# Moving one norm and thirteen projection steps earlier in a woven single-core transformer layer

## The chip, the cores and the metric

The kernel runs on one core of a Trainium2 chip. The metric is the device time of one execution in microseconds (us); the time of a kernel is the median of several executions. The engines are named as in the profile: PE (TensorE matmul) and PEld (its weight loads), DVE (VectorE), ACT (ScalarE), POOL (GpSimd, which here only issues gathers) and SP (SyncE, which issues all other transfers). An L and a number is a line of the kernel.

## The reference, cut to what matters

One layer over 1,024 tokens of width 1,024. The tokens are handled in blocks of 128, numbered 0 to 7.

```
xn     = rmsnorm(x, norm1_w)
proj   = xn @ w_in           # 52 column tiles of 128: q, k, v of two attentions, and two gates
o_d    = diff_attention(...) # 8 heads, two softmax maps each, chunk-causal
o_c    = chunk_attention(...)# 8 heads, band of 9 chunks of 64
merged = sigmoid(gd) * (o_d @ w_branch_diff) + sigmoid(gc) * (o_c @ w_branch_chunk)
h      = x + merged @ w_out
q      = rmsnorm(h, norm2_w) @ peer_wq       # then scores against two key tables
e, g   = the 16 best experts of 8 heads, and their softmax weights
y      = rmsnorm(h + sum_e g * gelu(u[e] . xn2) * v[e], final_norm_w)
```

## The kernel before, in words

Blocks are projected in two groups (L31): group 0 is blocks 0 and 1, group 1 is blocks 2 to 7 (768 tokens).

**Norm.** `norm1(gi, xp)` (L212) normalises a group block by block and yields after each. A block is one 512 KB load of `x` into a slot of the ring `wr`, a square with sum on ACT (L222), five tiny ACT operations for the reciprocal root (L113 to L118), a scaled copy (L224) into a slot of the ring `wl`, eight transposes on PE (L203), and eight pairs of an ACT copy (L231, `xh`) and a DVE subtraction (L232, `xl`), which split the value into a high and a low part.

**Projection steps.** `Dense` (L236) holds the 52 steps of a group. A step loads one 512 KB weight tile into `wr`, splits it on ACT (L126, `wh`) and DVE (L127, `wl`), multiplies it on PE in 24 products for every 512 tokens or part of them (L134; group 1 has a part of 512 and one of 256 tokens), copies the result on ACT into `st`, and SP stores it to DRAM (L287, L296, L302). `upto(n)` emits steps until n are emitted, `run()` emits one for each `next`. The ring `wr` has three slots and is shared by the norm's `x`, the steps' raw weights and the weights of the merges; `wh`, `wl` have two slots, `st` three.

**Attention.** `att_one` (blocks 0 and 1, one at a time) and `att_pair` (blocks 2 and 3) yield 12 and 24 times; they call `need`, which emits the projection steps that the next head needs, if they are not yet emitted. Attention reads k, v and q back from DRAM.

**Merge and selection.** `merge` (L478) yields 25 times: eight products with the two branch weights and gates (L505 to L511), eight with `w_out` and a transpose (L516 to L521), the second norm (L528 to L534), and eight query products with scores (L540 to L553) whose 16 best are found by DVE (`top16`, L558). `choose` (L565), called by `sel`, combines them on DVE in nine pieces and ends with the expert list `ei` of the block.

**Order.** `weave(main, n, (g, m))` (L52) advances `main` and, after its i-th piece, brings the side generator `g` to m * min(i, n) // n pieces; what is left of a side is emitted when `main` ends. The program order around the change is: norm of group 0; attention of block 0 woven with the rest of group 0's steps; merge of block 0 woven with attention of block 1; selection of block 0; merge of block 1 woven with the norm of group 1; selection of block 1; six steps of group 1; attention of blocks 2 and 3 woven with the other 46.

```
weave(merge(mp, 0, [0], yza, *ons[0]), 25, (att_one(wk, 1, yz1), 13))
run(sel([0], yza))
weave(merge(mp, 0, [1], yz1, *ons[1]), 25, (norm1(1, x1), 6))
...
run(sel([1], yz1))
```

Program order is not the order of issue. The kernel is built with a scheduler that runs a model of time over the whole program: an instruction that is earlier in the program goes first, and a later one whose inputs and buffers are there fills in. What comes out is a fixed order on each engine and queue. In the trace, for instance, gathers of `experts` (L790, called last of all) are issued by POOL between the pieces of merge 1.

**The rest.** Attention of blocks 4 to 7 with the merge of 2 and 3, gates and merges of the others, the selection of blocks 6 and 7, and then `dense_experts` (L681): blocks 2 to 5 go through all experts as 128 chunks of matrix products on PE. Blocks 0, 1, 6 and 7 (`experts`) gather 128 rows of `u` and 128 of `v` per block (L804, 512 KB each, five slots `ge`), which DVE reduces one by one (L810 for `u`, L816 for `v`).

## Time and profile before

| | us |
|---|---|
| time, median of three executions | 3437.65 (3435.08 to 3438.16) |
| the profiled execution, its own time | 3433.26 |
| its span, first to last instruction | 3431.5 |
| PE busy in the span | 3085.0 (90%) |
| DVE busy | 2700.0 (79%) |
| ACT busy | 1446.3 (42%) |
| POOL busy | 1249.1 (36%) |

The profiled execution is one of its own, some 4 us under the median of the three timed ones. A share of busy time is a mean over stages: PE has no idle time in some of them and waits in others. All positions in time below are us from the start of the span.

### The profile page before, as it was taken

What the parts mean: (1) busy time and instruction counts of PE and PEld (TensorE: products, weight loads), DVE (VectorE), ACT (ScalarE), POOL (GpSimd) and SP (SyncE); (2) the same over time, 40 slices, a digit from 0 to 9 for tenths busy, and PEclk for the clock granted to TensorE, in tenths of its full rate; (3) what the DMA queues carried; (4) which work ended last, traced back from release to release, by engine and by line L of the source; (5) the groups of instructions that cost most, each with busy time, mean ns of one, the idle gap of its engine ahead of it and who ended that gap; (6) DMA issues with size and microseconds to landing.
All of it is one profiled execution on the core that took longest, in us unless ns stands there. A gap on an engine that the chain in (4) does not pass through costs nothing.

```text
span 3431.5 us, 48288 instructions
## 1 busy us (share of the span) xinstructions
PE 3085.0 (90%) x16032; PEld 2551.8 (74%) x16032; DVE 2700.0 (79%) x5848; ACT 1446.3 (42%) x3029; POOL 1249.1 (36%) x1028
## 2 busy tenths in 40 slices
PE   7987699999979886987798359999999999999998
PEld 7986578888857654676677348888888888888886
DVE  4436897777779899987976978889998888999543
ACT  5634433434423544567669523333233333333332
POOL 0000455555544522344000144555555555555000
PEclk9999899999989987998898669999999999999999
DMA  7675999999999975898544499999999999999531
GB/s 240 219 244 189 374 333 348 333 352 334 326 340 351 324 236 186 281 360 331 203 162 157 145 343 319 346 350 339 347 345 345 346 342 344 346 340 349 166 123 49
DMA packets 406122, 987.13 MB, mean 288 GB/s; under 512 B 43184, under 2 KB 188400, under 8 KB 403696
## 3 DMA queue, kind: packets, MB, share of 16 engines
q0 software_dynamic: 147456, 536.94, 44.1%
q1 hardware_dynamic: 258416, 447.11, 37.4%
q8 instruction: 126, 2.06, 0.2%
q14 instruction: 124, 1.02, 0.1%
HBM read 905.72 MB, written 78.15 MB: 287 GB/s over the span
## 4 chain that ended last, share of the span: by engine, by line
PE 71%; issue 12%; DVE 7%; DMA 7%; ACT 2%; POOL 1%; SPq 0%; DVEq 0%; POOLq 0%; ACTq 0%
PE ph L134 20%; PE mm L134 16%; PE acc L710 15%; PE acc L717 5%; PE mm L490 5%; PE sc L347 3%; PE pv L372 3%; PE tr L203 2%; DMA ge<-in_u_dram,ei 2%; DVE junk L810 1%; DVE p L353 1%; POOL ge L804 1%; DMA rb<-rst 1%; DMA ge<-in_v_dram,ei 1%; DVE acc L816 1%
## 5 line engine op out<-in xcount | busy, mean ns | idle before, releaser
L804 POOL DMA_INDIRECT ge<-in_u_dram,ei x512 | 619.1, 1209 | 1249.0 <-DVE junk L810 396.4
L804 POOL DMA_INDIRECT ge<-in_v_dram,ei x512 | 629.8, 1230 | 683.2 <-DVE acc L816 462.0
L816 DVE SCALAR_TENSOR_TENSOR acc<-ge,a,acc 128x1024 f32<-128x1024 f32 x512 | 655.1, 1280 | 26.2 <-DMA ge<-in_v_dram,ei 20.1
L810 DVE SCALAR_TENSOR_TENSOR junk<-ge,xs 128x1024 bf16<-128x1024 f32 x512 | 624.7, 1220 | 53.7 <-DMA ge<-in_u_dram,ei 45.7
L127 DVE TENSOR_TENSOR wl<-wr,wh 128x1024 fp32r<-128x1024 f32 x232 | 283.6, 1223 | 233.1 <-ACT wh L126 107.5
L126 ACT CAST wh<-wr 128x1024 fp32r<-128x1024 f32 x232 | 243.7, 1051 | 406.5 <-PE ph L134 267.1
L134 PE MATMUL ph<-x2h,wh 128*128 128x512 f32 x1024 | 400.3, 391 | 11.8 <-ACT wh L126 10.4
L134 PE MATMUL ph<-x2l,wh 128*128 128x512 f32 x1024 | 399.9, 390 | 0.0
L134 PE MATMUL mm<-xh,wh 128*128 128x256 f32 (+1 forms) x1248 | 372.0, 325 | 0.7 <-ACT st L286 0.5
L134 PE MATMUL mm<-xl,wh 128*128 128x256 f32 (+1 forms) x1248 | 366.8, 321 | 1.4 <-DVE xl L232 1.3
L134 PEld LDWEIGHTS mm<-xh,wh 128*128 128x128 f32 x1248 | 236.9, 190 | 24.8 <-ACT st L286 2.3
L134 PE MATMUL ph<-x2h,wl 128*128 128x512 f32 x1024 | 253.1, 389 | 0.0
L134 PEld LDWEIGHTS mm<-xl,wh 128*128 128x128 f32 x1248 | 236.4, 190 | 21.5 <-DVE xl L232 2.1
L126 ACT CAST vh<-vr 128x512 fp32r<-128x512 f32 x256 | 140.4, 619 | 264.8 <-PE acc L717 243.4
L134 PE MATMUL mm<-xh,wl 128*128 128x256 f32 (+1 forms) x1248 | 234.4, 323 | 0.0
L134 PEld LDWEIGHTS ph<-x2h,wh 128*128 128x128 f32 x1024 | 193.2, 189 | 52.9 <-ACT wh L126 10.8
L134 PEld LDWEIGHTS ph<-x2l,wh 128*128 128x128 f32 x1024 | 193.2, 189 | 40.2
L134 PEld LDWEIGHTS ph<-x2h,wl 128*128 128x128 f32 x1024 | 192.3, 188 | 40.0
L347 PE MATMUL sc<-kt,qt 64*128 64x256 f32 (+3 forms) x608 | 202.1, 533 | 17.8 <-DVE mn L353 10.2
L710 PE MATMUL acc<-vh,ah 128*128 128x512 f32 x768 | 198.3, 389 | 0.0
L126 ACT CAST ah<-ge 128x512 fp32r<-128x512 f32 x128 | 79.7, 622 | 281.4 <-DVE ge L757 266.3
L134 PEld LDWEIGHTS mm<-xh,wl 128*128 128x128 f32 x1248 | 184.7, 189 | 16.8
(199 smaller groups left out, 5741.6 us busy)
## 6 DMA issues: line engine op xcount, KB each, us to landing
vr<-in_v_dram SPq DMA_DIRECT2D x128, 512.0 KB
wr<-in_ut_dram SPq DMA_DIRECT2D x128, 512.0 KB
wr<-in_w_in_dram SPq DMA_DIRECT2D x104, 512.0 KB
gdr<-gst SPq DMA_DIRECT2D x16, 2048.0 KB
gj<-gdr SPq DMA_DIRECT2D x512, 64.0 KB
wr<-in_w_bd_dram SPq DMA_DIRECT2D x40, 512.0 KB
wr<-in_w_out_dram SPq DMA_DIRECT2D x40, 512.0 KB
wr<-in_wq_dram SPq DMA_DIRECT2D x40, 512.0 KB
```

The lines of the kernel that those rows point to most:

```text
L126: nc.scalar.copy(hi, raw)
L127: nc.vector.tensor_sub(lo, raw, hi.bitcast(F32))
L134: nc.tensor.matmul(o, w[a][:, k, :], xx[b][:, k, :], start=(i == 0), stop=(i == last))
L203: nc.tensor.transpose(o[:, i * P:(i + 1) * P], s, ident)
L347: nc.tensor.matmul(o[:, :k1 - k0], q, k[:, k0:k1], start=True, stop=True)
L372: nc.tensor.matmul(o[:, :P], aT[:, j - c, :], vt[:, v0 + j, :], start=(j == 0), stop=(j == n - 1))
L490: nc.tensor.matmul(o, w[:, k, :], xx[:, k, :], start=(k == 0), stop=(k == K - 1))
L710: nc.tensor.matmul(acc[i][hf], a[x][:, i * P:(i + 1) * P], b[y][:, hf * 512:hf * 512 + 512], **kw)
L717: nc.tensor.matmul(o, aa[:, 3 * P:4 * P], bb[:, cs], start=(n == 0), stop=(n == len(todo) - 1))
L804: nc.gpsimd.indirect_dma_start(out=t, out_offset=None, in_=src, in_offset=bass.IndirectOffsetOnAxis(ap=ei[:, k:k + 1], axis=0))
L810: nc.vector.scalar_tensor_tensor(junk, t, 1.0, xs, op0=OP.mult, op1=OP.mult, accum_out=hid[:, k:k + 1])
L816: nc.vector.scalar_tensor_tensor(acc, t, a[:, k:k + 1], acc, op0=OP.mult, op1=OP.add)
```

## The change

`norm1(1)` is chained behind the remaining steps of group 0 as a side of block 0's attention, so its six blocks follow those steps (by the weave's counts two of them before that attention has ended and four when it has), instead of being spread over the merge of block 1. A new generator `some(n)` emits n steps, one per `next`. Group 1's steps come as sides: 2 over the merge of block 0, 4 over the selection of block 0, 3 over the merge of block 1 and 4 over the selection of block 1, which makes 13. The six steps ahead of `att_pair` fall away, and its side has 39 steps left instead of 46. Instructions, sizes, buffers and pools are the same as before; only the program order differs.

```diff
--- before.py
+++ after.py
@@ -262,6 +262,11 @@
             while self.done < min(n, len(self.steps)):
                 self.steps[self.done]()
                 self.done += 1
+
+        def some(self, n):
+            for _ in range(n):
+                self.upto(self.done + 1)
+                yield
 
         def run(self):
             while self.done < len(self.steps):
@@ -877,15 +882,14 @@
                 dn[0].upto(3)
                 setup()
                 dn[0].upto(6)
-                weave(att_one(wk, 0, yza), 13, (dn[0].run(), 46))
+                weave(att_one(wk, 0, yza), 13, (chain(dn[0].run(), norm1(1, x1)), 52))
             with pool("mp0") as mp:
-                weave(merge(mp, 0, [0], yza, *ons[0]), 25, (att_one(wk, 1, yz1), 13))
-                run(sel([0], yza))
-                weave(merge(mp, 0, [1], yz1, *ons[1]), 25, (norm1(1, x1), 6))
-            run(sel([1], yz1))
+                weave(merge(mp, 0, [0], yza, *ons[0]), 25, (att_one(wk, 1, yz1), 13), (dn[1].some(2), 2))
+                weave(sel([0], yza), 9, (dn[1].some(4), 4))
+                weave(merge(mp, 0, [1], yz1, *ons[1]), 25, (dn[1].some(3), 3))
+            weave(sel([1], yz1), 9, (dn[1].some(4), 4))
         with wpool("at1") as wk:
-            dn[1].upto(6)
-            weave(att_pair(wk, 1, yza), 25, (dn[1].run(), 46))
+            weave(att_pair(wk, 1, yza), 25, (dn[1].run(), 39))
     with pool("yzb") as yzb, pool("mp") as mp:
         d1 = [k for k in range(ND) if DBLK[k] < 4]
         d2 = [k for k in range(ND) if DBLK[k] >= 4]
```

## Rows read from the trace of the kernel before

**Rows 1.** The page: busy time per engine, and the granted clock in 40 slices.
```profile
PE 3085.0 (90%) x16032; PEld 2551.8 (74%) x16032; DVE 2700.0 (79%) x5848; ACT 1446.3 (42%) x3029; POOL 1249.1 (36%) x1028
...
PEclk9999899999989987998898669999999999999999
```

**Rows 2.** Busy by stretch: length, PE, PEld, DVE, ACT, POOL, clock, DMA share, GB/s.
```profile
195.00:435.00 240.00, 174.27 (x1194) 153.18 (x1195) 153.73 (x627) 98.76 (x297) 45.93 (x42) 0.88 0.79 278
...
960.00:1680.00 720.00, 615.99 (x3148) 460.52 (x3149) 637.76 (x1773) 386.40 (x924) 270.23 (x243) 0.90 0.84 296
1680.00:1925.00 245.00, 194.42 (x1066) 169.14 (x1066) 189.91 (x804) 177.65 (x408) 0.00 (x0) 0.87 0.44 158
...
2010.00:3190.00 1180.00, 1169.55 (x5146) 967.85 (x5147) 1048.30 (x1372) 370.62 (x558) 616.61 (x482) 0.99 0.96 343
...
340.00:435.00 95.00, 56.29 (x357) 50.56 (x356) 75.70 (x246) 41.38 (x117) 45.32 (x42) 0.82 0.97 370
...
519.00:960.00 441.00, 440.68 (x2602) 369.40 (x2600) 334.75 (x512) 173.78 (x370) 236.51 (x193) 1.00 0.95 339
```

**Rows 3.** What PE waited for from 195 to 435 us: total us, times, longest.
```profile
PE tr L203 <- ACT xs L224: 18.3, 4, 7.1
PE tr L203 <- DVE xs L530: 10.6, 2, 6.5
PE mm L490 <- DMA wr<-in_w_bd_dram: 7.2, 5, 2.9
PE sc L547 <- ACT st L542: 6.7, 4, 5.1
```

**Rows 4.** Timeline of PE: first products of two successive projection steps; first of att_pair.
```profile
473.60 0.39 PE L134 MATMUL mm<-xh,wh 128*128 128x512 f32 x1
...
482.02 0.39 PE L134 MATMUL mm<-xh,wh 128*128 128x512 f32 x1
...
519.41 1.77 PE L347 MATMUL sc<-kt,qt 64*128 64x384 f32 x6
```

**Rows 5.** Timeline of PE: sixteen equal products of merge 1 at two clocks.
```profile
322.56 2.02 PE L490 MATMUL mm<-on,wr 128*128 128x128 f32 x16 [1.72 <-DVE ohib L617]
...
328.41 3.65 PE L490 MATMUL mm<-on,wr 128*128 128x128 f32 x16 [2.93 <-DMA wr<-in_w_bd_dram]
```

**Rows 6.** Groups of instructions by form, 325 to 453 us: busy us, mean ns, idle before.
```profile
L231 ACT ACTIVATE xh<-tr,w1c 128x128 fp32r<-128x128 f32 x48 | 16.9, 367 | 28.2 <-DVE xl L232 22.3 <-PE tr L203 4.0 <-issue 1.2
...
L232 DVE SCALAR_TENSOR_TENSOR xl<-tr,w1c,xh 128x128 fp32r<-128x128 f32 x48 | 15.6, 343 | 3.9 <-ACT xh L231 3.3 <-issue 0.2
...
L224 ACT ACTIVATE xs<-xt,nr 128x1024 f32<-128x1024 f32 x6 | 6.9, 1148 | 0.2
L222 ACT ACTIVATE xs<-xt 128x1024 f32<-128x1024 f32 x6 | 6.3, 1058 | 6.9 <-DMA xt<-in_x_dram 6.8
...
L114 ACT ACT_TABLE_LOAD x1 | 1.3, 1283 | 0.0
```

**Rows 7.** What SP's queue waited for: 300 to 435 us (first row), 435 to 600 us.
```profile
SPq L487 <- ACT xs L224: 13.4, 4, 3.8
...
SPq L287 <- ACT st L286: 36.2, 13, 9.5
SPq L296 <- ACT st L292: 17.9, 4, 5.9
```

**Rows 8.** Line L804 (the gathers) by stretch; line L810; POOL's last instruction.
```profile
435.00:960.00 525.00, 280.81 (x228) 1.00 0.95 338
960.00:1680.00 720.00, 270.23 (x243) 0.90 0.84 296
...
L810 DVE SCALAR_TENSOR_TENSOR junk<-ge,xs x512: 1196/1220/1280, 346.4 to 2888.4; 128x1024 bf16<-128x1024 f32 x171
L810 DVE DVE_READ_ACCUMULATOR junk<-ge,xs x512: 70/82/89, 347.5 to 2889.6; 128x1 f32 x171
...
3180.41 1.14 POOL L804 DMA_INDIRECT ge<-in_v_dram,ei  x1 [2.99 <-DVE acc L816]
```


## The prediction

> **What bounds the kernel now.** I read the page first: PE is busy nine tenths of the span, DVE eight, and the granted clock leaves full speed only in some slices [rows 1]. So the question is where PE waits. The table of busy time by stretch answers it [rows 2]. From 519 to 960 us, while group 1 is projected, PE has no gap (440.68 of 441 us), and the dense experts from 2010 to 3190 us are full too (1169.55 of 1180). Between them lie stretches in which PE is idle a seventh to a fifth of the time. The change touches the first stretch with gaps, 195 to 435 us, in which blocks 0 and 1 are merged and selected: PE is busy 174.27 of 240 us, so 65.7 us idle, and 38.7 of these lie in the last 95 us (340 to 435), where merge 1, the norm and the first gathers run together. What ended these gaps stands in [rows 3]: first the norm's own transposes, for which PE stands 18.3 us until ACT has scaled the block; then the second norm of the merges (10.6), weights of the first products on their way (7.2), and the query copies on ACT (6.7). The gap belongs to the path: what follows, 519 to 960 us, is PE without a hole, so a microsecond of projection that fits into a gap ahead of it is a microsecond less there. At the far end nothing takes it away: POOL's last gather is issued at 3180 us [rows 8], 250 us before the end of the span, and PE's dense chunks are the last to finish.
>
> **The change part by part.** *The thirteen steps.* One step of group 1 takes PE 8.42 us: the first product of one stands at 473.60 us, that of the next at 482.02 us [rows 4]. Nine steps (2 + 4 + 3) come ahead of the end of merge 1, so 9 x 8.42 = 75.8 us of PE work is added to the stretch with the gaps, and the same 75.8 us leaves the full stretch behind it. The last four, over selection 1, replace the six that stood there before and ran under the same DVE work; that exchange I cost at nothing, since the steps left over for the attention of blocks 2 and 3 fill PE as soon as their buffers are free, as they do now until the first product of that attention at 519.41 us [rows 4]. If that cover is gone, PE waits for the end of selection 1, at most two steps, 17 us. So the gain is the part of the 65.7 us of gaps that the nine steps fill, between 0 (they only lengthen the stretch by 75.8) and 65.7.
>
> *How much is filled.* The 18.3 us at the norm's transposes I count in full: the transposes no longer stand in PE's queue among merge 1's products. Of the other 47.4 us I take half, 23.7. Speaking for more: the steps interleave product by product with whatever is ready. Against: PE's order is fixed by a model of time, and gaps that the model does not foresee (late weights, DVE held by a gather) stay gaps whatever is placed behind them. Sum 42.0.
>
> *The clock.* The stretch has a mean granted clock of 0.82 to 0.88, against 1.00 in the full ones [rows 2]. Sixteen equal products of merge 1 take 2.02 us behind a short wait and 3.65 us behind a long one [rows 5], the first at the level of 2.4 GHz, the second mostly at 1.2. Each such case costs 1.6 us. The mean of 0.88 over 240 us is about 58 us at the lower level, mostly gaps; if a seventh of it is work, 8 us are lost. I take 4 of them back; bounds 0 and 8.
>
> *The norm, moved.* It leaves merge 1: 30.1 us of ACT (L231 16.9, L224 6.9, L222 6.3) and 15.6 us of DVE [rows 6]. It also leaves the ring `wr`: SP held merge 1's weights 13.4 us until L224 had let go of a slot [rows 7], which is part of the waits for weights above and not counted again. DVE in that last stretch is busy 75.7 of 95 us, so three steps there, 3 x 1.2 us of splitting, are less than what goes. In its new place the norm lies beside the end of block 0's attention and the start of merge 0. ACT is busy 98.8 of 240 us in the whole stretch, so 30 us more are hidden there; PE has merge 0's products to do meanwhile. If the cover is gone, PE waits for four blocks of about 5 us of ACT each (30.1 / 6), 20 us; I take 0, since four such blocks fit into ACT's idle time beside merge 0.
>
> *The function tables.* A load of ACT's tables takes 1283 ns, and in merge 1 the six norms share one, at L114 [rows 6]. Beside the exponentials of attention each may need two, 12 x 1.283 = 15.4 us of ACT, between 0 and that, inside the 141 us that ACT has idle, so nothing is added to the sum. The Trainium skill speaks against the move here: "ScalarE: Activation LUTs", section "Table sets: the hidden batching unit", says to batch calls by table set, and its section "What ACT_TABLE_LOAD costs" gives 2.66 us per switch with the drain. By that figure 12 switches are an estimated 32 us of ACT; were all of it on the path, the gain would fall to about 9 us, and the load itself agrees with the trace (1283 ns).
>
> *SP's queue.* Each moved step issues one load and two or three stores, and the stores wait for ACT. With the steps in the full stretch SP waited 36.2 us in 13 waits at L287 and 17.9 in 4 at L296 [rows 7], 3.2 us each, with the next weights queued behind. There PE does not notice, since its own work is what is late. In merge 1 the weights behind such a store would be the merge's. With three slots of `wr` in flight I take 0; this is the third rival.
>
> *Given back later.* The gathers of blocks 0 and 1 start when selection 0 ends. Two steps and part of four come before that, so about 25 us later, while the main work arrives 41 us earlier: 66 us less for gathers under the full stretch. At 228 in 525 us [rows 8] that is 29 gathers, and 29 x 1.3 us (1.22 us at L810 and 0.08 for its readout [rows 8]) = 38 us of DVE work, which goes to later stretches. From 960 to 1680 us DVE is busy 637.76 of 720 us, from 1680 to 1925 only 189.91 of 245 with no gather at all [rows 2]. So there is room for it; PE is idle 14% of the first stretch, with gathers, and 21% of the second, without, so the rows show no price of a gather as such. I take 5 us, bounds 0 and 38.
>
> *Sum:* 42.0 + 4 - 5 = 41 us less. Against the profiled execution's own 3433.26 us that is 3392; against the median of 3437.65 us it is 3397, which I give.
>
> **The rivals.** *First: little is filled.* The fixed order puts a step's products ahead of merge products that would be ready, or PE waits for `wl` because DVE stands behind a gather. Only the norm's 18.3 us are won, less 5: 3424 us. For it: in 340 to 435 us the DMA share is 0.97, so what is late there is late for every load. Against: a step needs 0.9 MB (512 KB in, 384 KB out) for 8.4 us of PE, a merge's tile 512 KB for 2 us, so the steps thin the demand out.
>
> *Second: given back.* All 38 us of displaced gathers land on the path in 960 to 1680 us, where DVE is nearly full: 42 + 4 - 38 = 8 us gained, 3430. For it: DVE at 89% there. Against: the empty stretch behind it.
>
> *Third, on the other side: SP's stores hold up the merges.* Nine steps bring some 20 stores; at 3.2 us each that is 64 us in which the next weights are not issued. If half of it, 32 us, reaches PE as new gaps and nothing but the norm's 18.3 us is won, with 5 given back, the change costs 32 - 18.3 + 5 = 19 us: 3456. It decides from the point where PE's idle time in the merges and selections, plus what is given back, grows beyond the 65.7 us of now. Against: in a stretch where PE has gaps the copies that the stores wait for come soon after their products.
>
> **How the numbers follow.** The forecast, a gain of 20 to 66 us (3372 to 3418), has a chance of 0.62; a still larger gain (everything filled and 8 us of clock) 0.04; little filled 0.14; given back 0.10; stores in the way or some other new wait 0.10. A measurement of this kernel tells about 0.2%, 7 us, from no change. Faster: 0.62 + 0.04 + most of 0.14 = 0.78. Given back and the rest of little filled are the same: 0.12. Slower 0.10. The range leaves out the slower case and the largest gains: 3366 to 3434.
>
> **What would show it.** Right: a norm transpose (tr from xs) before some 230 us and none waiting among merge 1's products; projection products among those of the merges; PE's idle time from 195 us to the first product of `att_pair` down from 66 to 20 to 30 us; that first product later than 519.41 us by 20 to 40 us, yet the last projection product some 40 us earlier than 960; the dense chunks starting as much earlier. Wrong: the same idle time spread differently, waits of SP for `st` with PE waiting for `wr` behind them, or a gain at 960 us that is gone at 2010 us with DVE busier and PE idler between. The prediction fails most simply if the model's order lets the steps displace the merges instead of filling their gaps.

## The result, and the profile after

The changed kernel takes 3468.89 us (median of 4 runs, 3466.28 to 3477.31) where the kernel before took 3437.9 us on the same chip: a ratio of 1.0089 (95% interval 1.0072 to 1.0106), 31 us slower. The prediction was 41 us faster. Its profiled execution has a span of 3467.6 us, 36 more than before.

The page: busy time per engine and the granted clock, to be set against [rows 1]. PE has 13 us more of busy time for the same 16032 products.
```profile
PE 3097.7 (89%) x16032; PEld 2555.8 (74%) x16032; DVE 2703.9 (78%) x5848; ACT 1450.2 (42%) x3037; POOL 1249.8 (36%) x1028
...
PEclk9989989899999986899998769999999999999999
```
Busy by stretch, the columns of [rows 2]: first stretches that answer to those rows, then the stages of the changed kernel by its own marks (end of the attention of block 0; merge 0; selection 0; merge 1; selection 1).
```profile
195.00:435.00 240.00, 186.44 (x1172) 159.61 (x1171) 131.39 (x481) 104.58 (x292) 33.65 (x32) 0.87 0.68 226
519.00:960.00 441.00, 413.03 (x2353) 341.97 (x2351) 356.25 (x658) 164.58 (x351) 242.65 (x193) 0.96 0.95 334
960.00:1680.00 720.00, 621.08 (x3185) 462.24 (x3185) 628.25 (x1642) 366.26 (x873) 288.17 (x252) 0.89 0.86 301
2010.00:3190.00 1180.00, 1139.81 (x5011) 943.34 (x5012) 1043.66 (x1389) 363.93 (x548) 619.07 (x489) 0.98 0.96 342
...
195.00:223.00 28.00, 11.42 (x37) 6.58 (x36) 10.95 (x41) 26.26 (x67) 0.00 (x0) 0.58 0.57 177
223.00:335.00 112.00, 95.97 (x666) 84.70 (x666) 47.81 (x212) 56.73 (x174) 0.00 (x0) 0.91 0.64 202
335.00:389.00 54.00, 51.18 (x301) 42.94 (x300) 41.00 (x169) 20.35 (x48) 9.29 (x9) 1.00 0.53 175
389.00:519.00 130.00, 93.13 (x591) 83.49 (x589) 91.39 (x218) 15.71 (x43) 62.70 (x60) 0.86 1.00 377
519.00:616.00 97.00, 71.21 (x385) 60.28 (x385) 88.69 (x259) 24.74 (x44) 51.89 (x43) 0.88 0.93 326
```
The stretch from 195 to 435 us did get 12 us more of PE work (186.44 against 174.27 in [rows 2]); a reader who stops there would call the change a success. By the stages of the work, as both traces mark them, it is none:

| stage (us) | before: length, PE idle, steps | after: length, PE idle, steps |
|---|---|---|
| 195 to merge 0's first product | 4.9, 2.3, 0 | 28.0, 16.6, 0 |
| to merge 1's first product | 98.6, 13.4, 0 | 166.3, 18.9, 6.0 |
| to merge 1's last query product | 126.8, 42.6, 0 | 129.6, 36.9, 2.0 |
| to the first product of `att_pair` | 94.2, 9.2, 9.3 | 96.7, 25.8, 7.5 |
| to the last projection product | 440.0, 0.0, 42.7 | 396.7, 2.2, 36.5 |
| to the first dense product | 1059.6, 243.0 | 1040.3, 232.1 |

PE's idle time from 195 us to the last projection product rose from 67.5 to 100.4 us. That product came at 1012.3 us instead of 959.4, 53 us late; the next stage gave 19 back, so the dense experts started 34 us late (2052.6 against 2019.0), and from there to the end both take the same (1412.5 and 1415.0 us).

What PE waited for from 195 to 435 us, as in [rows 3], and from 545 to 1013 us: total us, times, longest.
```profile
PE mm L495 <- DMA wr<-in_w_bc_dram: 11.5, 5, 3.6
PE tr L203 <- DVE xl L232: 8.9, 3, 3.3
PE mm L495 <- DMA wr<-in_w_bd_dram: 7.0, 5, 2.9
...
PE tr L203 <- ACT xs L224: 3.1, 1, 3.1
...
PE sc L352 <- DMA qt<-qd: 22.9, 2, 20.7
```
The 18.3 us behind L224 are 3.1 now, as predicted. In their place PE waits for merge 1's weights, for the norm in its new place (L232) and, once for 20.7 us, for the queries of `att_pair`. The timeline (PE, SP, DVE) shows that last wait:
```profile
593.65 1.32 PE L134 MATMUL mm<-xh,wl 128*128 128x512 f32 x5
615.67 3.49 PE L352 MATMUL sc<-kt,qt 64*128 64x384 f32 x7 [20.70 <-DMA qt<-qd]
...
603.26 0.33 SPq L326 DMA_DIRECT2D kt<-kd  x1
...
602.89 0.22 DVE L624 TENSOR_TENSOR sel<-ohib 128x64 f32<-128x64 bf16 x1
```
PE ends its last queued step at 595 us. The first key load of `att_pair` is issued at 603.26 us, 0.15 us after DVE has last read the tile `ohib` of selection 1 (602.89 + 0.22); by the trace SP waited 9.7 us for this L624. The load's tile comes from a pool that is opened after the pool of `ohib` has been closed, so it may lie in the same memory. PE has no step left to bridge the wait. In [rows 4] the same product stands at 519.41 us.

ACT from 195 to 223 us, groups by form: busy us, mean ns, idle before. ACT has no idle time to speak of there, and five of its instructions are table loads.
```profile
L231 ACT ACTIVATE xh<-tr,w1c 128x128 fp32r<-128x128 f32 x16 | 5.5, 359 | 0.5 <-DVE xl L232 0.4
L224 ACT ACTIVATE xs<-xt,nr 128x1024 f32<-128x1024 f32 x4 | 4.6, 1143 | 0.0
L222 ACT ACTIVATE xs<-xt 128x1024 f32<-128x1024 f32 x3 | 3.1, 1048 | 0.0
...
L114 ACT ACT_TABLE_LOAD x2 | 2.6, 1283 | 0.0
...
L365 ACT ACT_TABLE_LOAD x2 | 2.6, 1283 | 0.0
...
L306 ACT ACT_TABLE_LOAD x1 | 1.3, 1283 | 0.0
```
What SP's queue waited for from 375 to 545 us, as in [rows 7]:
```profile
SPq L492 <- PE mm L495: 37.6, 19, 4.0
SPq L292 <- ACT st L291: 15.9, 5, 7.3
...
SPq L301 <- ACT st L297: 10.8, 2, 8.8
```
Gathers issued (POOL, L809) up to the last projection product, as in [rows 8]: 285, where before 270 had been issued by 959.4 us. Of the 512 of blocks 0 and 1, 227 are then left instead of 242.
```profile
0.00:1012.30 1012.30, 345.04 (x285) 0.94 0.84 292
```

### The profile page after: what moved, and what is told of

The parts are those of the page before. It is cut to its first block, busy times and chain, and to the rows that moved or that the text cites. A ratio compares the mean times of both kernels' runs of the same rounds, so it can differ in the third digit from the quotient of the medians.

```text
span 3467.6 us, 48293 instructions
## 1 busy us (share of the span) xinstructions
PE 3097.7 (89%) x16032; PEld 2555.8 (74%) x16032; DVE 2703.9 (78%) x5848; ACT 1450.2 (42%) x3037; POOL 1249.8 (36%) x1028
## 4 chain that ended last, share of the span: by engine, by line
PE 67%; issue 14%; DMA 8%; DVE 6%; ACT 3%; POOL 2%; SPq 0%; DVEq 0%; POOLq 0%; ACTq 0%
PE ph L134 20%; PE mm L134 15%; PE acc L715 15%; PE acc L722 5%; PE mm L495 4%; DMA ge<-in_u_dram,ei 3%; PE sc L352 3%; PE pv L377 3%; PE tr L203 2%; POOL ge L809 2%; DVE junk L815 1%; DVE acc L821 1%; DMA ge<-in_v_dram,ei 1%; DVE p L358 1%; DMA qt<-qd 1%
## 5 line engine op out<-in xcount | busy, mean ns | idle before, releaser
L809 POOL DMA_INDIRECT ge<-in_u_dram,ei x512 | 612.6, 1197 | 1302.3 <-DVE ei L644 709.1
L809 POOL DMA_INDIRECT ge<-in_v_dram,ei x512 | 636.9, 1244 | 665.4 <-DVE acc L821 410.5
L352 PE MATMUL sc<-kt,qt 64*128 64x256 f32 (+3 forms) x608 | 212.9, 543 | 42.6 <-DMA qt<-qd 30.3
## 6 DMA issues: line engine op xcount, KB each, us to landing
gdr<-gst SPq DMA_DIRECT2D x16, 2048.0 KB
```

The costliest lines, as they stand in the source:

```text
L352: nc.tensor.matmul(o[:, :k1 - k0], q, k[:, k0:k1], start=True, stop=True)
L809: nc.gpsimd.indirect_dma_start(out=t, out_offset=None, in_=src, in_offset=bass.IndirectOffsetOnAxis(ap=ei[:, k:k + 1], axis=0))
```

## The experiments

Marks of every kernel (us), each the start of an instruction. "Last" is the last projection product, "left" the gathers of blocks 0 and 1 not yet issued then, "dense" the first dense product. The marks come from one profiled execution each, and executions of one kernel differ: the 23 of the kernel before on one of the chips took 3430.9 to 3446.3 us. The ratio is to the kernel before on the same chip, with its 95% interval; the intervals reach 3 to 9 us to either side.

| kernel | merge 0 first, last query | first gather | merge 1 starts, takes | att_pair | last | left | dense | ratio |
|---|---|---|---|---|---|---|---|---|
| before | 199.9, 293.2 | 339.4 | 298.5, 126.8 | 519.4 | 959.4 | 242 | 2019.0 | 1 |
| after | 223.0, 335.0 | 375.5 | 389.3, 129.6 | 615.7 | 1012.3 | 227 | 2052.6 | 1.0089 (1.0072 to 1.0106) |
| e1_norm_alone | 225.1, 327.2 | 368.6 | 332.1, 97.5 | 525.6 | 971.5 | 246 | 2048.1 | 1.0063 (1.0044 to 1.0082) |
| e2_norm_woven | 237.3, 338.9 | 382.3 | 394.9, 134.5 | 624.1 | 1023.7 | 223 | 2078.8 | 1.0170 (1.0152 to 1.0189) |
| e3_four_more | 222.9, 334.3 | 374.7 | 388.6, 131.8 | 621.6 | 981.8 | 244 | 2041.7 | 1.0051 (1.0034 to 1.0068) |
| e4_sel0_free | 225.6, 336.6 | 378.9 | 349.9, 112.5 | 558.0 | 981.7 | 244 | 2051.8 | 1.0085 (1.0058 to 1.0111) |
| e5_own_bufs | 205.2, 330.7 | 374.0 | 387.4, 132.4 | 613.0 | 1012.1 | 227 | 2060.8 | 1.0097 (1.0080 to 1.0113) |
| e6_one_root | 219.8, 334.5 | 377.1 | 391.0, 129.8 | 612.5 | 1010.1 | 227 | 2048.0 | 1.0087 (1.0066 to 1.0108) |
| e7_norm_merge0 | 202.0, 319.4 | 369.3 | 376.4, 127.8 | 600.2 | 977.2 | 243 | 2038.4 | 1.0046 (1.0031 to 1.0061) |
| e8_two_more | 200.3, 294.0 | 340.0 | 299.2, 126.6 | 520.6 | 960.8 | 242 | 2021.4 | 0.9991 (0.9978 to 1.0003) |
| e9_held_before | 199.5, 293.1 | 444.2 | 298.3, 104.3 | 458.3 | 935.9 | 289 | 2055.7 | 1.0130 (1.0109 to 1.0151) |
| e10_held_after | 224.2, 335.6 | 520.2 | 389.9, 90.7 | 529.1 | 934.7 | 324 | 2062.6 | 1.0153 (1.0132 to 1.0174) |
| e11_norm_wide | 201.3, 294.3 | 343.3 | 299.1, 126.0 | 523.7 | 965.4 | 240 | 2016.2 | 0.9988 (0.9976 to 0.9999) |
| e12_both_trims | 223.1, 333.0 | 375.6 | 346.3, 117.2 | 565.2 | 961.2 | 257 | 2036.9 | 1.0042 (1.0022 to 1.0062) |
| e13_norm_sel1 | 200.1, 292.9 | 334.8 | 297.9, 97.7 | 515.6 | 1001.4 | 220 | 2045.0 | 1.0075 (1.0055 to 1.0095) |
| e14_less_pe | 199.5, 297.2 | 344.3 | 302.8, 129.7 | 526.6 | 922.6 | 266 | 2008.4 | 0.9972 (0.9958 to 0.9985) |
| e15_less_dve | 199.7, 294.1 | 339.3 | 299.2, 124.8 | 503.0 | 955.8 | 241 | 2010.9 | 0.9959 (0.9946 to 0.9972) |
| e16_own_merge1 | 200.2, 300.1 | 346.9 | 303.8, 114.5 | 518.2 | 962.6 | 240 | 2024.4 | 0.9988 (0.9979 to 0.9998) |
| e17_own_wide | 201.8, 300.5 | 344.1 | 304.3, 111.4 | 521.2 | 963.8 | 239 | 2025.3 | 0.9997 (0.9984 to 1.0010) |
| e18_trims_wide | 226.6, 335.5 | 377.7 | 348.9, 113.8 | 564.6 | 962.0 | 256 | 2038.3 | 1.0041 (1.0028 to 1.0054) |

### The change in parts: e1 to e4

**e1_norm_alone** is the kernel before with the norm alone moved.
```diff
-weave(att_one(wk, 0, yza), 13, (dn[0].run(), 46))
+weave(att_one(wk, 0, yza), 13, (chain(dn[0].run(), norm1(1, x1)), 52))
...
-weave(merge(mp, 0, [1], yz1, *ons[1]), 25, (norm1(1, x1), 6))
+run(merge(mp, 0, [1], yz1, *ons[1]))
```


> Only the norm is moved behind group 0's steps; every projection step of group 1 stays where it was before the change. Theory A (the norm's new place is what costs: between 195 and 240 us PE loses about 21 us of gaps and 10 us of clock to a saturated ACT, and selection 1's tail is no longer covered): the loss of about 30 us is there without any early step and merge 1 gives 18 us back, so some 3440 to 3455 us. Theory B (the early steps over selection 0 push merge 1 behind selection 0 and wholly under the gathers, the norm is harmless): faster than before the change by 10 to 20 us, 3418 to 3428. Theory C (the stores of the early steps hold SP's queue): as B, since no step is early.

3460.78 us, ratio 1.0063: the norm's new place alone is 22 of the 31 us (15 to 28 by the interval). That is theory A's side, above its range of 3440 to 3455 us; theories B and C, both faster than before, are out. Merge 0 starts 25 us late and takes 9 more, the first gather comes 29 us late, and merge 1 gives 29 us back (97.5 for 126.8). So merge 1 ends only 4 us late, the last projection product 12, but the dense experts 29.

**e2_norm_woven** is the changed kernel with the norm woven into block 0's attention from its start, beside the steps of group 0.
```diff
-weave(att_one(wk, 0, yza), 13, (chain(dn[0].run(), norm1(1, x1)), 52))
+weave(att_one(wk, 0, yza), 13, (dn[0].run(), 46), (norm1(1, x1), 6))
```


> The changed kernel, with the six norm blocks woven evenly between group 0's last 46 steps instead of chained behind them, so that PE has products to do while ACT scales the blocks. Theory A: the gaps between 195 and 240 us go, 20 to 30 us less than the changed kernel, 3439 to 3449. Theories B and C: within 8 us of the changed kernel's 3469.

3495.3 us, the slowest of all, which none of the theories forecast. The norm there takes slots of `wr` and `wl` from group 0's steps: from 50 to 195 us SP held weight loads (L194) 9.4 us for the norm's L232 and 3.1 us for its L224, waits that the kernel before does not have there. PE, which was full in that stretch, is busy 131.54 of 145 us, and merge 0 starts at 237.3 us.

**e3_four_more** is the changed kernel with four more steps queued ahead of `att_pair`.
```diff
+dn[1].upto(17)
-weave(att_pair(wk, 1, yza), 25, (dn[1].run(), 39))
+weave(att_pair(wk, 1, yza), 25, (dn[1].run(), 35))
```


> The changed kernel, with four more steps emitted between selection 1 and the attention of blocks 2 and 3 (17 done, 35 left as its side). Theory A, second half: PE no longer stands 20.7 us at the first scores of that attention, because its queue holds 34 us of products ahead of them; 15 to 21 us less than the changed kernel, 3448 to 3454. Theories B and C: within 8 us of the changed kernel's 3469.

3455.77 us, 13 less than the changed kernel (theory A asked for 15 to 21). The wait of 20.7 us is gone, PE's idle time in that stage falls from 25.8 to 4.9 us, and the last projection product comes 30 us earlier; 20 of these are given back by the dense start, with 244 gathers left instead of 227.

**e4_sel0_free** is the changed kernel without its four steps over selection 0.
```diff
-weave(sel([0], yza), 9, (dn[1].some(4), 4))
+run(sel([0], yza))
```


> The changed kernel without the four steps over selection 0 (they go to the side of the attention of blocks 2 and 3, 43 left). Theory B: merge 1 runs beside selection 0 again and its first products come before the gathers, 20 to 30 us less than the changed kernel, 3439 to 3449. Theory A: the four steps filled gaps; without them PE idles beside selection 0 and the time is the changed kernel's 3469 or up to 15 us more. Theory C: four steps fewer, about 10 stores at 3.2 us, up to 15 us less, 3454.

3465.53 us, no measurable difference from the changed kernel. Theory B was right that merge 1 moves ahead, and wrong about the time. Merge 1 starts 39 us earlier and takes 112.5 us instead of 129.6, the last projection product comes 31 us earlier, and 30 of these are given back before the dense start.

### The price of the norm: e5, e6, e7, e13

**e5_own_bufs** takes the norm's tiles out of the shared rings.
```diff
-xt = wp.tile([P, KC, P], F32, name="xt", tag="wr", bufs=WBUFS) ...
+xt = gp.tile([P, D], F32, name="xt", tag="ge") ...   # group 1 only
-xs = wp.tile([P, KC, P], F32, name="xs", tag="wl") ...
+xs = gp.tile([P, D], F32, name="xs", tag="ge") ...   # group 1 only
```


> The changed kernel, with the six blocks of the second norm (x and the scaled copy) in the five gather buffers, which stand empty until selection 0, instead of the rings of weights and weight halves that group 0's last steps still use. In the changed kernel the first product of merge 0 stands at 223.0 us, 23 later than before. Theory A, ACT is what the norm waits for (ACT was busy 26.26 of the 28 us from 195 to 223): the rings are not the cause, the first product of merge 0 stays within 4 us of 223, the time within 8 us of 3469. Theory B, the norm waits for slots of the shared rings: its first blocks move ahead into the attention of block 0, merge 0 starts at 210 us or earlier, and the time is about 3455 us.

Theory B has merge 0's start right (205.2 us: four blocks of the norm are now scaled from 25 to 53 us) and the time wrong (3473.56). Merge 0 then takes 125.5 us, and its last query stands at 330.7 us, 4 earlier than in the changed kernel. The start of merge 0 is thus not what sets its end. What stayed in its place is the rest of the norm: its transposes stand from 199 to 250 us, in the changed kernel from 199 to 254.

**e6_one_root** takes one root for the six blocks.
```diff
+for i, b in enumerate(GROUPS[1]):          # x loaded, squares summed
+    nc.scalar.activation(xs, xt, AF.Square, accum_out=sall[:, i:i + 1])
+rall = rsqrt(sm, sall, 6, 1.0 / D)
...
-r = rsqrt(sm, ss, 1, 1.0 / D)
+r = rall[:, i:i + 1]
```


> The changed kernel, with the sums of squares of all six blocks of the second norm taken first and one reciprocal root for the six, so that ACT changes its tables once or twice there instead of ten times; x is read a second time for the scaled copies (3 MB more to load). Theory A, ACT and its tables make the toll: eight or more loads of 1.283 us and five roots less are some 10 to 18 us of ACT, merge 0 starts at 205 to 213 us instead of 223, and the time falls by about as much, to 3452 to 3460 us. Theory B, the rings or the order make it: merge 0 starts at 220 us or later (the second reading of x takes ring slots too), and the time is 3469 us or more.

ACT's table loads from 140 to 300 us, in the changed kernel (first fence) and in this one:
```profile
L114 ACT ACT_TABLE_LOAD x5 | 6.4, 1283 | 0.0
L365 ACT ACT_TABLE_LOAD x3 | 3.8, 1283 | 0.1
L306 ACT ACT_TABLE_LOAD x2 | 2.6, 1283 | 0.0
```
```profile
L114 ACT ACT_TABLE_LOAD x2 | 2.6, 1283 | 0.0
L317 ACT ACT_TABLE_LOAD x1 | 1.3, 1283 | 0.0
L376 ACT ACT_TABLE_LOAD x1 | 1.3, 1283 | 0.0
```
Ten loads became four, merge 0 starts 3 us earlier, and the time is the same (3468.06 us). Theory A falls: the tables are not a price of 10 us or more. A saving of a few microseconds could be hidden by the second reading of x.

**e7_norm_merge0** weaves the norm over merge 0, with no step there and 15 queued ahead of `att_pair`.
```diff
-weave(att_one(wk, 0, yza), 13, (chain(dn[0].run(), norm1(1, x1)), 52))
+weave(att_one(wk, 0, yza), 13, (dn[0].run(), 46))
...
-weave(merge(mp, 0, [0], yza, *ons[0]), 25, (att_one(wk, 1, yz1), 13), (dn[1].some(2), 2))
+weave(merge(mp, 0, [0], yza, *ons[0]), 25, (att_one(wk, 1, yz1), 13), (norm1(1, x1), 6))
...
+dn[1].upto(15)   # and 37 steps as the side of att_pair
```


> The norm of group 1 is woven over merge 0 (beside block 1's attention) instead of following group 0's projections; no step in merge 0, four over selection 0, three over merge 1, four over selection 1, then four more before the attention of blocks 2 and 3. Theory A, what the norm costs depends on the work that PE has beside it: merge 0 starts at 200 us again, its last query stands at 300 to 312 us (6 us of transposes, little more), PE waits under 25 us from 195 us to the end of merge 1 beyond what merge 1 itself waits, and the time is 3410 to 3430 us, faster than both. Theory B, the toll of 20 us of ACT and tables is paid wherever the norm stands outside merge 1: the last query of merge 0 at 320 us or later, and 3445 us or more.

3454.21 us, near theory B: at 319.4 us the last query is 26 us later than before. ACT is busy 71.87 of merge 0's 117.40 us, against 35.31 of 93.30 before.

**e13_norm_sel1** is the kernel before with the norm over selection 1.
```diff
-weave(merge(mp, 0, [1], yz1, *ons[1]), 25, (norm1(1, x1), 6))
-run(sel([1], yz1))
+run(merge(mp, 0, [1], yz1, *ons[1]))
+weave(sel([1], yz1), 9, (norm1(1, x1), 6))
```


> The kernel before with the norm of group 1 over selection 1, behind merge 1, instead of over merge 1; no step moved. The first gather stays at 339 us. Theory A, the time follows DVE's idle time up to the first dense product (460 us before, 489 in the changed kernel): merge 1, without the norm, ends some 20 us earlier, PE then waits for the norm, DVE has gathers to reduce meanwhile and is idle no longer than before: first dense product within 10 us of 2019, time 3427 to 3447 us. Theory B, PE's gaps are the path: PE has nothing to do for some 30 us of norm and selection, the last projection product stands at 970 us or later, and the time is 3447 us or more.

Windows of merge 1 and of what follows it up to `att_pair`, and, in a fence of its own, what PE waited for in the second:
```profile
297.90:395.50 97.60, 71.35 (x514) 64.89 (x515) 69.22 (x269) 19.39 (x55) 27.78 (x26) 0.91 0.84 306
395.50:515.60 120.10, 59.94 (x258) 45.99 (x257) 108.07 (x331) 54.54 (x130) 54.66 (x52) 0.66 0.84 292
```
```profile
PE tr L203 <- DVE xl L232: 38.4, 7, 11.8
```
Merge 1 gains 29 us, and PE then loses 60 of 120 us, because DVE, which must clear the norm's transposes, is busy 108.07 of 120.10 us with selection and gathers. 3463.62 us: theory B.

### The gathers: e9, e10, and what is queued: e8, e12

**e9_held_before** and **e10_held_after** let no gather start before selection 1 has ended, in the kernel before and in the changed one.
```diff
...                  # block 0's ef in a tile of its own
-nc.vector.tensor_copy(ei, ef.rearrange("p a b -> p (a b)"))
+if b == 0:
+    held.append((ei, ef))
+else:   # e0 = f0 + 0 * ef: waits for selection 1
+    for e0, f0 in held:
+        nc.vector.scalar_tensor_tensor(e0, ef ..., 0.0, f0 ..., op0=OP.mult, op1=OP.add)
+    nc.vector.tensor_copy(ei, ef.rearrange("p a b -> p (a b)"))
```


> The kernel before, with the row numbers of block 0 written only when selection 1 has ended (the same numbers, through one more DVE operation that also reads selection 1's), so that no gather runs beside merge 1. Theory A, merge 1 is held up by the gathers' loads (DMA share 0.98 from 345 to 435 us): merge 1 takes about 100 us instead of 126.8, the last projection product stands at 920 to 940 us instead of 959, and the gathers that come later (about 45) lengthen the stage from there to the first dense product by about as many times 1.2 us, to 1100 us or more; the time is 3435 to 3470 us. Theory B, merge 1 is held up by the norm's chain alone: 120 us or more, last projection product above 950 us.

> The changed kernel with the same hold: no gather before selection 1 has ended. Theory A, the steps over merge 1 fill nothing there because the loads of merge 1, of the steps and of the gathers share a DMA that is full (share 1.00, 377 GB/s from 389 to 519 us): without gathers merge 1 with its steps takes 100 us or less instead of 129.6, PE's idle time in it falls from 36.9 to under 15 us, and the last projection product stands at 985 us or earlier instead of 1012. Theory B, PE's fixed order holds the steps behind merge products that wait for ACT and DVE: the idle time stays above 25 us and merge 1 above 115 us.

Windows of merge 1 in e9, then of merge 1 and of selection 1 in e10:
```profile
298.30:402.60 104.30, 78.07 (x555) 71.53 (x555) 60.26 (x292) 50.87 (x141) 0.00 (x0) 0.89 0.59 194
```
```profile
389.90:480.70 90.80, 79.53 (x588) 72.13 (x586) 27.00 (x121) 17.74 (x47) 0.00 (x0) 0.98 0.65 210
480.70:529.10 48.40, 48.40 (x278) 40.99 (x276) 37.50 (x155) 19.95 (x35) 5.47 (x6) 1.00 0.48 159
```
Theory A in both, for the stage: the changed kernel's merge 1, with the same steps, the same order and the same stores, takes 90.7 us instead of 129.6, and PE's idle time in it falls from 36.9 to 11.3 us (90.80 - 79.53). The hold takes the gathers' loads and their reductions on DVE out of merge 1 together. By the waits of PE there, the loads are the larger part: what it waits for the merge's own weights falls from 23.7 to 7.0 us, what it waits for DVE from 8.3 to 1.9. The last projection product comes 23 and 78 us earlier. And both kernels are slower for it, 3479.63 and 3487.6 us: 47 and 97 more gathers are left, and the stage up to the dense start is 60 and 88 us longer, 1.28 and 0.90 us for each. The upper end of 3470 us that e9's expectation gave was passed.

The traces show where the stage grows most. Its parts before the merge of blocks 6 and 7 and after that merge's last query product take 817 to 840 us together in all kernels of the table, in no order by the gathers left. The merge itself took 230.9 us before, with no gather of blocks 0 and 1 left to issue, and takes 286.2 us in e9 with 45 of them and 295.2 us in e10 with 79. Its windows, in the kernel before and in e9:
```profile
1671.40:1902.20 230.80, 186.58 (x1034) 162.99 (x1033) 175.71 (x726) 165.20 (x382) 0.00 (x0) 0.88 0.45 161
```
```profile
1652.60:1938.90 286.30, 199.83 (x1053) 171.30 (x1052) 229.99 (x777) 168.08 (x388) 52.21 (x46) 0.82 0.61 217
```
DVE has 54 us more of work there, its idle time stays (55 and 56 us), and what PE waits for DVE there grows from 24.5 to 57.5 us: the merge got longer by what DVE was given. In all kernels but e10 (27 us) DVE is idle 51 to 58 us in this merge, whether it takes 218 us or 286. Of the 19 us by which the changed kernel's stage is shorter than before, 9 lie in this merge and 10 in the other parts.

**e8_two_more** (the kernel before, `upto(8)` for `upto(6)`):

> The kernel before with eight instead of six steps of group 1 behind selection 1's start, and nothing else. Before, PE had used up its queued steps and stood 9.2 us ahead of the first product of the attention of blocks 2 and 3 at 519.4 us. Theory A, a microsecond of projection put into that gap is a microsecond less at the last projection product (959.4 us before, now about 951), and 0 to 8 us less at the end: 3428 to 3437 us. Theory B, the steps only push the scores back and the gap stays: 959 and 3437 us, or more.

3438.15 us, theory B: the scores come 1.2 us later and the gap is 10.2 us instead of 9.2.

**e12_both_trims** is e4 with 13 steps queued ahead of `att_pair`:
```diff
-weave(sel([0], yza), 9, (dn[1].some(4), 4))
+run(sel([0], yza))
...
+dn[1].upto(13)
```


> The changed kernel without the four steps over selection 0 and with the same number of steps queued as before ahead of the attention of blocks 2 and 3 (13 of them done there). Each of the two alone moved the last projection product from 1012 to 982 us. If they remove different waits (18.3 us at the scores, 30 us of PE time ahead of merge 1), they add up: the last product at 955 to 970 us, the time 3445 to 3460 us, since the stage after it gives back 1.2 us for every gather that is then left. If both remove the same wait, the last product stays at about 980 us and the time at 3456 to 3466 us.

They add up: 961.2 us and 3450.68 us. This is the most telling comparison with the kernel before. The last projection product stands where it stood (961.2 and 959.4), but the first gather came 36 us later, 15 gathers more are left, and the dense experts start 18 us later; the time is 14 us above by the ratio (1.0042).

### Whose time counts: e14, e15

**e14_less_pe** and **e15_less_dve** take work from PE alone and from DVE alone, in the kernel before.
```diff
-todo = [(k, 0, b) for k in range(K) for b in range(2)] + [(k, 1, 0) for k in range(K)]
+todo = [(k, 0, b) for k in range(K) for b in range(2)]       # e14: gate steps of group 1
...
-nc.vector.scalar_tensor_tensor(junk, t, 1.0, xs, ...)
+n = D // 2 if b == 0 and k % 2 else D                        # e15
+nc.vector.scalar_tensor_tensor(junk[:, :n], t[:, :n], 1.0, xs[:, :n], ...)
```


> The kernel before with a third of PE's products left out in the 16 gate steps of group 1 (those with the remainder of the weights, so gates of lower precision; ACT, DVE and loads are as before). This takes 16 thirds of 8.42 us, 45 us, from PE. Theory A, DVE sets the first dense product: the last projection product comes some 45 us earlier (959 to about 915), yet the first dense product moves by less than 12 us from 2019 and the time is 3425 us or more. Theory B, PE is the path up to there: first dense product at 1970 to 1985 us and the time 3390 to 3405 us.

> The kernel before, in which every second of block 0's 128 first reductions takes only half of its columns (so those sums are incomplete; the gathers and PE's work are as before). This takes 64 times about 0.6 us, 39 us, from DVE. Theory A, DVE sets the first dense product: it comes 28 to 39 us earlier than 2019 us, and the time is 3398 to 3410 us. Theory B, PE is the path: the last projection product stays at 959 us, the first dense product within 10 us of 2019 and the time at 3428 us or more.

The first dense product on PE's timeline, in e14 and in e15 (2019.02 us before):
```profile
2008.45 0.80 PE L134 MATMUL ph<-x2h,wh 128*128 128x512 f32 x1 [9.99 <-ACT wh L126]
```
```profile
2010.91 0.79 PE L134 MATMUL ph<-x2h,wh 128*128 128x512 f32 x1 [10.37 <-ACT wh L126]
```
e14 meets theory A's marks for the dense start and the time (3429.18 us), e15 meets theory B's but for the time (3424.62 us, below 3428), so as accounts of both runs neither theory holds. 46 us less of PE (3085.0 to 3039.0 us) bring the last projection product 37 us forward and the dense start 11; with 24 more gathers left the stage between is 26 us longer. The time falls by 10 us. In e15 DVE's busy time up to the dense start falls by 32 us (1559 to 1527), the dense start comes 8 us earlier, and the time falls by 14.

e15 says less of DVE than it was meant to. All but 1.4 us of its saving stands ahead of the last projection product, while PE projects; there DVE is busy 621.23 us instead of 652.19, and yet the gathers get no further (241 left, 242 before). In the stage behind it, where the gathers that are left are paid, DVE has as much to do as before:
```profile
959.40:2019.00 1059.60, 816.60 (x4240) 634.43 (x4238) 907.00 (x2840) 581.84 (x1360) 308.05 (x275) 0.85 0.73 258
```
```profile
955.80:2010.90 1055.10, 813.54 (x4240) 631.10 (x4238) 905.60 (x2838) 579.90 (x1360) 316.83 (x274) 0.86 0.74 259
```
What less work for DVE in that stage would bring, no run here shows.

### Looking for a version that beats both: e11, e16 to e18

**e11_norm_wide**, in the kernel before:
```diff
-for j in range(4):                       # 4 copies on ACT, 4 remainders on DVE
-    ...
+t = cols4(xs[:, 512 * g:512 * g + 512], 4)
+nc.vector.tensor_tensor(t, cols4(o, 4), w1c[:, cs].unsqueeze(2).to_broadcast([P, 4, P]), op=OP.mult)
+split(t, xh[:, cs, i * P:(i + 1) * P], xl[:, cs, i * P:(i + 1) * P])
```


> The kernel before, with the norm's 48 scaled copies on ACT and 48 remainders on DVE per group done in 12 wider pieces (128x512: one product by the weights on DVE, one copy on ACT, one remainder on DVE); the numbers are the same. If the norm's ACT work sets its price (L231 16.9 us of the norm's 30.1 us of ACT in merge 1), merge 1 gets 5 to 15 us shorter than 126.8, and the time is 3422 to 3435 us. If it is the gathers' loads and DVE that set merge 1's length, merge 1 stays at 122 us or more and the time at 3437.

**e16_own_merge1** gives the norm's x two tiles of its own in the kernel before (a pool `nx` beside `mp0`), **e17_own_wide** both, and **e18_trims_wide** is e12 with the wide norm.

> The kernel before, the norm over merge 1 as it was, but its x in two tiles of its own instead of slots of the ring of weights. Before, SP held merge 1's weights 13.4 us until the norm had let go of a slot. Theory A, the ring is most of the norm's price in merge 1: merge 1 takes 108 to 116 us instead of 126.8, the last projection product stands at 945 to 952 us, and, with about two thirds given back by gathers that are then left, the time is 3428 to 3434 us. Theory B, the price is ACT's, DVE's and the full DMA's: merge 1 at 122 us or more and the time at 3435 to 3440 us.

> The run before with the norm's copies and remainders also in 12 wide pieces instead of 48. Alone these wide pieces gave 3433 us (ratio 0.9988). Theory A: both add up, merge 1 at 100 to 112 us, 3422 to 3430 us, below both kernels. Theory B: no more than the wide pieces alone, 3431 to 3438 us.

> The changed kernel without the steps over selection 0 and with 13 steps queued ahead of the attention of blocks 2 and 3 (3450.7 us), now with the norm in 12 wide pieces. Theory A, ACT's instructions set the wait ahead of merge 0 (ACT 26 of 28 us busy there): merge 0 starts at 210 to 216 us instead of 223, the first gather comes 8 to 15 us earlier than 375.6, and the time is 3438 to 3445 us. Theory B, they do not: merge 0 at 220 us or later, 3448 us or more.

e11: 3433.41 us, merge 1 at 126.0, though ACT is busy 43.2 us in it instead of 51.0: the norm's ACT time does not set merge 1's length. e16: 3433.15 us; SP no longer waits for L224, merge 1 takes 114.5 us, but merge 0 takes 6.6 more, since two blocks of the norm are now done there, the first gather comes 7.5 us later, and the last projection product 3. e17 is 3436.63 us, no sum of the two. e18 is 3453.45 us with merge 0 at 226.6 us: theory B. So e11 and e16 are ahead of the kernel before by 0.12%, less than the 0.2% that was called telling, and nothing with the norm moved reaches it.

## Why the prediction was wrong

Two steps that the prediction put at nothing cost the most: the norm's move (22 us, e1) and the exchange over selection 1 (13 us, e3). The term that was to pay for them, filled gaps for 42.0 us, did not come: PE's idle time from 195 us to the last projection product rose by 33 us.

**The bound.** "What follows, 519 to 960 us, is PE without a hole, so a microsecond of projection that fits into a gap ahead of it is a microsecond less there" is true of the last projection product and not of the time. e10 brought that product 78 us forward from the changed kernel and lost 19 us. While PE projects, the gathers of blocks 0 and 1 run on DMA and DVE, and what they have not done by then is done in the stage up to the dense experts. Over all kernels but e15 (whose reductions are shorter) that stage grows by 0.92 us per gather left, with a scatter of up to 14 us (a line through the 19 points of the table). Full PE was read as sole path; e14 shows that it is not, and e9 and e10 that gathers that come later lengthen the stage behind.

**How much is filled** (42.0 us of 65.7). The wait for the norm's transposes went, as said. Of the other gaps little was filled, for a reason that is in the table of stages: six of the steps ran ahead of merge 1, five of them between the last query of merge 0 and merge 1's first product. Before, merge 1 ran under selection 0, and these two products stood 5 us apart with 1.5 us idle; now they stand 54 us apart, with PE busy for 51. So steps were put where there was no gap. Merge 1 so began 14 us after the first gather instead of 41 us before it, and its loads met the gathers' (share of DMA 1.00 at 377 GB/s); its idle time fell only from 42.6 to 36.9 us. That the gathers are what holds merge 1 there is shown by e10; that it is mostly their loads, by the waits beside it. The prediction had named the cause, "in 340 to 435 us the DMA share is 0.97", for its first rival, and answered that steps thin the demand out; they need loads too.

**The norm, moved** (taken 0, bound 20): the term with the largest share. Merge 0's start is 25 us late in e1, merge 0 itself 9 us longer. What merge 1 wins by it is 29 us, more than the 18.3 us counted, but it is won behind the first gather, and the first gather is 29 us late. The cover named, ACT's idle time in 195 to 435 us, is a mean over a stretch: in the 28 us ahead of merge 0, where four of the norm's six blocks are scaled, ACT was busy 26.26. What in the norm makes merge 0 end late is not settled: without its ring slots (e5), with six table loads fewer (e6) or with wide pieces (e18) the last query of merge 0 stayed at 331 to 336 us.

**The function tables** (taken 0): right as far as e6 tells. Ten loads of 1283 ns instead of four cost nothing that it could measure. By the 2.66 us per switch of the Trainium skill ("ScalarE: Activation LUTs", section "What ACT_TABLE_LOAD costs") six fewer would be an estimated 16 us of ACT; merge 0's start moved by 3. In the trace the next instruction follows a load at once (load 200.64 to 201.92 us, the next at 201.93).

**The exchange over selection 1** (taken at nothing; "at most two steps, 17 us" if the cover were gone): the cover was gone, the wait was 20.7 us. With the wait removed the time falls by 13 us (e3). The load of the first tiles waited for the end of selection 1, and the queued steps did not last until then.

**The clock** (4 us): not there. 0.87 from 195 to 435 us against 0.88, and 0.96 from 519 to 960 us against 1.00. Its bound was mis-sized too: a seventh of 58 us at the lower level is 8 us of work, which would take 4 at the full clock, so that 4 us are lost there and not 8.

**SP's queue** (taken 0; third rival, 3456 us, the sign that came true). SP did wait 26.7 us for stores' copies (15.9 + 10.8), but these waits are not what made merge 1 long: while merge 1 ran, SP waited 21.8 us for ACT at these stores in the changed kernel and 20.4 us in e10, whose merge 1 is 39 us shorter. The rival's end came true by luck; its mechanism is not what the runs show.

**Given back later** (taken 5, bounds 0 to 38): its mechanism was real and weighed more than was taken: it decided how much of a shift at 960 us reached the time. Its sign turned, because the main work came later, not earlier: 15 gathers fewer were left and 19 us came back. In e3 20 of 30 us, in e4 30 of 31 and in e14 26 of 37 were given back. The room that the prediction saw, 189.91 us of DVE in 245 from 1680 to 1925 us, was not free: gathers that reach into the merge of blocks 6 and 7 lengthen it (e9).

**The sum as measured.** The norm's place 22 us (e1); the wait ahead of `att_pair` 13 us (e3 against the change); with both trims the remaining five steps over the merges bring 8 us (e12 against e1: 14 for 22 us). 22 + 13 - 8 = 27 of 31 us; the four steps over selection 0 are within what can be told (e4). Each term has an error of 6 to 10 us by the intervals, so the 8 us are hardly told from nothing, and the agreement of the sum is partly luck. Open stays why e1 loses 17 us between the last projection product and the dense start with only four gathers more left, which by 0.92 us would be 4; 7 of them lie in the merge of blocks 6 and 7 (238.2 us for 230.9), into which three gathers reach.

## What to carry to other kernels

A full engine is not yet the path: ask what else advances beside it, and what is left of that when it ends early; here 46 us off PE were worth 10. Room on an engine in a later stage is not free until a run has filled it: DVE idle for 55 us in a merge kept that idle time, and the merge grew. Before work is moved ahead of a stage, see what that stage was ahead of: the moved steps put merge 1 behind the start of the gathers and delayed that start itself. Idle time of the covering engine is to be read in the few microseconds where the moved piece will stand, not over the whole stretch.

## What was not expected of the hardware

One and the same merge took 126.8 us with the norm and the gathers beside it, 97.7 with the gathers alone (e13) and 104.3 with the norm alone (e9): two neighbours that cost 22 and 29 us when the other is there. PE's own products did not take the same time either: those of merge 1 are 67.2 us of PE in the changed kernel and 57.5 us in e10. Their time goes with the granted clock of the stretch (0.86 and 0.98) and not with the gathers: without gathers but with the norm (e9) they are 62.7 us at 0.89, with gathers but without the norm (e13) 61.1 us at 0.91.
